# A feed-forward block in seven-product form: weight sums written as additions, part of them done by accumulating DMA

## The chip, the cores and the metric

One core of one Trainium2 chip runs the whole kernel. The metric is the device time in microseconds (us) of one execution; shorter is better. The engines are named as in the profile: PE (TensorE, matmuls), DVE (VectorE), ACT (ScalarE), POOL (GpSimd), SP (SyncE, which here only issues DMAs). A DMA that adds to what lies at its destination (accumulating DMA) is issued from POOL.

## The reference

A decoder layer over 1024 tokens of width 1024, in float32. What matters here is its last third:

```python
x = x + y @ w_out
h = rmsnorm(x, ffn_norm_g)
x = x + (silu(h @ w_gate) * (h @ w_up)) @ w_down     # 1024 -> 2816 -> 1024
return rmsnorm(x, final_norm_g)
```

Every operand of a matmul is split into a high part (rounded to the float32r format of PE) and a low part (the rest), and three matmuls high*high, high*low, low*high replace one in float32.

## The kernel before

**Seven products instead of eight.** The products `h @ w_gate` and `h @ w_up` are cut in blocks of two by two: rows in two halves of 512, the inner width in two halves, and two column blocks of 128 of the weight. The 2816 columns give 11 such pairs of blocks (`HF` = 11, index `j`), each once for gate and once for up (`m`). Each pair is done with seven block products instead of eight. That needs sums and differences of the weight blocks a11, a12, a21, a22 and of the row blocks. Class `Seven` (L694) does it: `load_part` loads the raw blocks (tile `wr`: half `kh` = 0 holds a11 and a21, half 1 holds a12 and a22), `mix` (L733) makes the weight sums on POOL, `prep` (L747) makes the high and low part of one operand (tile `wl`; high by ACT, low by DVE, in `split`, L160 and L161), and `run` (L772) issues the 12 matmuls of one product and combines its result on ACT or DVE. For a pair, `mix` computes

```python
add(s[:, 0, k], a21[:, k], a22[:, k], eng_)          # operand of product 5
sub(s[:, 1, k], s[:, 0, k], a11[:, k], eng_)         # operand of product 6
sub(a21[:, k], a11[:, k], a21[:, k], eng_)           # operand of product 7
```

(tile `sm` is `s`), and `prep` of product 7 takes `s[:, 1]` from a12 in place, which is product 3's operand. The products stand in the order 1, 6, 2, 7, 5, 4, 3; for the first two pairs it is 1, 2 of pair 0, 1, 2 of pair 1, then 6, 7, 5, 4, 3 of pair 0, then of pair 1 (`head`, L1489). In the trace product 6 is `fb<-t2h,wl`, 7 is `fb<-t3h,wl`, 5 `fa<-t1h,wl`, 4 `fb<-t4h,wl`, 3 `fa<-b22h,wl`, 1 `fa<-b11h,wl` and 2 `fa<-b21h,wl`. After product 7 the sum in `s[:, 1]` is no longer needed and its place takes an intermediate result (`sm<-fb,pu`).

**The rows.** The normalized rows come in eight blocks of 128; `to_h` (L1428) transposes a block and, for blocks 4 to 7, forms the differences with blocks 0 to 3: `r[:, 0]` (t1), `t23` (t2 and t3), and `r[:, 1]` (t4; tile `hraw`), the last by a POOL subtraction. `rest` inside it and `late_split` (L1556) make their high and low parts.

**What sets the order.** From L1606 to L1673 PE, DVE, ACT and POOL run in the order in which the code is written (`manual_schedule`); after that, and for SP throughout this stretch, a scheduler orders the instructions. The written order interleaves `prep_to(n)` (operands up to number n), `run()`, and the row work:

```python
    for i in range(1, 5):
        late_split(i - 1)
        if i == 2:
            ffn.prep_to(11)
        if i == 3:
            ffn.prep_to(12)
        ffn.run()
    ffn.prep_to(14)
    ffn.mix(1)
```

Tiles `wr`, `wl`, `sm`, `wd`, `act`, `hraw` and `t23` share 21 slots of 4 KB per partition (`U`); the raw weights of pairs 1 and up lie in slots of 8 KB (`V`). `wd_out` (L1508) loads blocks of `w_down`, forms differences on POOL and stores them; `act_out` (L1493) does the same with the activations.

Of the kernel before, what the change touches and what calls it, by code (L numbers as in the profile page):

```python
# [89 lines left out]
def hybrid_block_kernel(  # L90
# [603 lines left out]
    class Seven:  # L694


        def __init__(self, pairs, ms, load, done, ahead, load_at, mix_at, head=(), at=None, scale=None, scale_at=(), piece=4):
# [109 lines left out]
    def load_gate(j, kh):  # L807
        t = U("wr", F32, (P, 4, 2, P))
        nc.sync.dma_start(t, w_gt[j, kh])
        return {"g": t}  # L810

    def scale_gate(j, kh, k, raw):
        t = raw["g"]
        g = gT[:, 4 * kh + k:4 * kh + k + 1]
        if j == 0:
            nc.vector.tensor_scalar(t[:, k], t[:, k], g, None, op0=ALU.mult)  # L816
        else:
            nc.scalar.activation(t[:, k], t[:, k], AF.Copy, scale=g)
# [658 lines left out]
    def ffn_done(j, m, ps, f, sh, other):  # L1477
# [3 lines left out]
        if other is not None:  # L1481
            add(other, ps, other, nc.vector)
# [3 lines left out]
        else:  # L1486
# [383 lines left out]
```

## Time and profile before

| | |
|---|---|
| times of three runs | 1359.94, 1364.36, 1359.34 us, median 1359.94 |
| the profiled execution | 1360.19 us, its span 1358.4 us |
| PE | 1331.8 us busy, 98% of the span |
| DVE / ACT / POOL | 944.6 / 653.4 / 596.2 us, 70% / 48% / 44% |
| granted PE clock | 0.999 of full speed |

The span runs from the first to the last instruction; the execution's time has 1.8 us more around it. A matmul's end is modelled, so the pace of PE is read from the starts of matmuls. A row of a timeline gives start, duration, engine, line, operation, output and inputs, and in brackets the idle time of the engine just before it and what ended it.

### The profile page before, as it was taken

Reading aid. Unit: us, or ns where it says so; the run is one execution under the profiler, and the core shown is the slowest. Engines: PE = TensorE matmul, PEld = TensorE weight load, DVE = VectorE, ACT = ScalarE, POOL = GpSimd, SP = SyncE. Lnnn points to the kernel's source line nnn. Section 1 sums busy time; section 2 is a strip of 40 time slices with the busy share of each in tenths; the row PEclk is TensorE's granted clock in tenths of the full one; section 3 lists DMA queues with packets and bytes.
Section 4 is the critical chain, followed back from the end, with each engine's and each line's share of the span. In section 5 each row is a group of like instructions: output and inputs, shape, how many; then the busy total and the mean of one; then the engine's idle time right before and its main releaser. Section 6 shows DMA issues by size and latency. Waiting matters only on the chain.

```text
span 1358.4 us, 18967 instructions
## 1 busy us (share of the span) xinstructions
PE 1331.8 (98%) x6552; PEld 1112.0 (82%) x6552; DVE 944.6 (70%) x1527; ACT 653.4 (48%) x1317; POOL 596.2 (44%) x636
## 2 busy tenths in 40 slices
PE   9999999999999999999999999999999999999997
PEld 6899878878788888888887788888888888888886
DVE  6868767776777887489878866666656664664862
ACT  7433667665567777654357232322332332644452
POOL 1115545553066555131045875766665541022521
PEclk9999999999999999999999999999999999999999
DMA  9454332335100111598041353645444425996503
GB/s 360 161 182 154 115 106 82 98 121 174 71 2 13 43 32 32 219 307 264 31 171 62 112 188 140 227 178 178 147 153 165 163 85 184 379 385 237 171 16 140
DMA packets 78239, 205.39 MB, mean 151 GB/s; under 512 B 8768, under 2 KB 15424, under 8 KB 77504
## 3 DMA queue, kind: packets, MB, share of 16 engines
q1 hardware_dynamic: 76848, 199.99, 41.5%
q0 software_dynamic: 1152, 4.19, 1.6%
q8 instruction: 52, 0.85, 0.3%
q14 instruction: 43, 0.35, 0.1%
q10 hardware_dynamic: 144, 0.00, 0.0%
HBM read 141.24 MB, written 59.77 MB: 148 GB/s over the span
## 4 chain that ended last, share of the span: by engine, by line
PE 72%; DVE 7%; ACT 4%; issue 3%; POOL 3%; DMA 0%; POOLq 0%; ACTq 0%; DVEq 0%
PE fa L169 7%; PE fa L167 7%; PE fa L168 7%; PE fd L168 5%; PE fd L167 5%; PE fd L169 5%; PE fb L167 5%; PE fb L169 5%; PE fb L168 5%; DVE wl L161 2%; PE pTb L1161 2%; PE xo L167 1%; PE xo L168 1%; PE xo L169 1%; PE oA L167 1%
## 5 line engine op out<-in xcount | busy, mean ns | idle before, releaser
L161 DVE TENSOR_TENSOR wl<-wr,wl 128x512 fp32r<-128x512 f32 x150 | 154.6, 1052 | 75.4 <-ACT wl L160 75.1
L161 DVE TENSOR_TENSOR lrv<-lr,lrv 128x1024 fp32r<-128x1024 f32 x77 | 105.0, 1396 | 49.7 <-ACT lrv L160 47.1
L160 ACT CAST lrv<-lr 128x1024 fp32r<-128x1024 f32 x77 | 80.1, 1052 | 96.3 <-PE fd L169 56.0
L169 PE MATMUL fd<-lrv 128*128 128x512 f32 x308 | 119.9, 389 | 0.0
L168 PE MATMUL fd<-lrv 128*128 128x512 f32 x308 | 119.9, 389 | 0.0
L167 PE MATMUL fd<-lrv 128*128 128x512 f32 x308 | 119.9, 389 | 0.0
L172 POOL TENSOR_TENSOR wr<-wr,sm 128x512 f32<-128x512 f32 (+1 forms) x38 | 46.8, 1241 | 121.2 <-DVE wl L161 115.1
L160 ACT CAST wl<-wr 128x512 fp32r<-128x512 f32 x150 | 87.3, 623 | 3.1 <-DVE wr L816 2.6
L161 DVE TENSOR_TENSOR wl<-sm,wl 128x512 fp32r<-128x512 f32 x60 | 55.2, 946 | 45.4 <-ACT wl L160 45.4
L295 POOL TENSOR_SCALAR ms<-ss 128x1 f32<-128x1 f32 x32 | 9.8, 305 | 140.4 <-ACT xn L1582 62.5
L1146 POOL TENSOR_TENSOR denb<-denb,neg_one 128x1 f32<-128x1 f32 x64 | 36.4, 570 | 75.0 <-ACT p L1145 64.3
L167 PEld LDWEIGHTS fd<-lrv 128*128 128x128 f32 x308 | 57.8, 188 | 12.1
L169 PEld LDWEIGHTS fd<-lrv 128*128 128x128 f32 x308 | 57.8, 188 | 12.0
L168 PEld LDWEIGHTS fd<-lrv 128*128 128x128 f32 x308 | 57.8, 188 | 11.9
L1145 ACT ACTIVATE p<-scb,nmb 128x384 f32<-128x384 f32 (+3 forms) x64 | 47.5, 743 | 36.8 <-DVE nmb L1144 35.0
L161 DVE TENSOR_TENSOR ptl<-pTb,pth 128x512 fp32r<-128x512 f32 (+2 forms) x96 | 50.0, 549 | 13.6 <-ACT pth L160 12.8
L1144 DVE CUSTOM_DVE_ANT_0 scb<-scb,mask 128x384 f32<-128x384 f32 (+3 forms) x64 | 48.5, 758 | 14.1 <-PE scb L1136 13.7
L1485 ACT ACTIVATE act<-sm 128x512 f32<-128x512 f32 x11 | 7.0, 633 | 103.7 <-DVE sm L175 103.7
L1147 POOL TENSOR_SCALAR p<-p,denb 128x384 f32<-128x384 f32 (+3 forms) x64 | 49.1, 768 | 6.3
L1485 ACT ACTIVATE act<-pu 128x512 f32<-128x512 f32 x22 | 13.9, 632 | 74.8 <-DVE pu L175 74.8
L160 ACT CAST pth<-pTb 128x512 fp32r<-128x512 f32 (+2 forms) x96 | 42.9, 482 | 13.5 <-PE pTb L1161 12.9
L169 PE MATMUL fa<-t1h,wl 128*128 128x512 f32 x120 | 46.8, 391 | 2.6 <-DVE wl L161 2.6
(354 smaller groups left out, 4374.8 us busy)
## 6 DMA issues: line engine op xcount, KB each, us to landing
lr<-la_d SPq DMA_DIRECT2D x77, 256.0 KB, 5.4
wr<-in_w_gate_dram SPq DMA_DIRECT2D x22, 512.0 KB, 4.3
wr<-in_w_up_dram SPq DMA_DIRECT2D x22, 512.0 KB, 5.0
wd<-in_w_down_dram SPq DMA_DIRECT2D x22, 512.0 KB, 6.4
rb_d<-wd SPq DMA_DIRECT2D x22, 512.0 KB, 2.6
la_d<-sd SPq DMA_DIRECT2D x22, 512.0 KB, 4.8
lr<-rb_d SPq DMA_DIRECT2D x44, 256.0 KB, 5.4
lr<-in_w_down_dram SPq DMA_DIRECT2D x33, 256.0 KB, 5.6
```

Of the source, the lines that this page charges most:

```text
L160: nc.scalar.copy(hi, src)
L161: (eng or nc.vector).tensor_tensor(lo, src, hi.bitcast(F32), op=ALU.subtract)
L167: nc.tensor.matmul(ps, ah, bh, start=first and i == 0, stop=False, skip_group_check=go_on)
L168: nc.tensor.matmul(ps, ah, bl, start=False, stop=False, skip_group_check=go_on)
L169: nc.tensor.matmul(ps, al, bh, start=False, stop=last and i == n - 1, skip_group_check=go_on)
L172: eng.tensor_tensor(out, a, b, op=ALU.subtract)
L1144: nc.vector.tensor_tensor_reduce(s_, s_, m_, 1.0, -NEG, op0=ALU.add, op1=ALU.min, accum_out=nm)
L1145: nc.scalar.activation(p_, s_, AF.Exp, scale=-1.0, bias=nm, accum_out=den)
L1146: nc.gpsimd.tensor_tensor(den, den, neg_one[:, 0:1], op=ALU.pow)
L1147: nc.gpsimd.tensor_scalar(p[:, 0:w], p[:, 0:w], den, 0.0, op0=ALU.mult, op1=ALU.add)
L1161: nc.tensor.transpose(pp[:, i], p[:, blk(k0 + i)], ident)
L1485: nc.scalar.activation(dst, src, AF.Silu)
```

## The change

In the feed-forward block (`plus=True`) every weight sum is written as an addition: s1 = (a21 + a22) + a11, a21 + a11, a12 + s1. The signs move to the rows' operands and to the combinations of results. Accumulating DMAs then do a part of the work: (1) `r[:, 1]` of the row blocks 4 to 7; (2) for pair 0 (its mix stays on POOL) the sums a12 + s1; (3) for pair 1 all sums: SP loads a21 from DRAM into both halves of `sm`, then a22 and a11 are added from DRAM, and s1 to a12 from SBUF. Pairs 2 to 10 keep POOL. The weights' layout is changed so that a block is contiguous in a partition, for the feed-forward block and for the gates, which use the same class. The calls are put in another order.

```diff
     class Seven:
...
         def part(self, j, m, kh, f):
             self.load_part(j, kh)
             self.scale_part(j, kh)
-            return self.raws[(j, kh)][m][:, :, f]
+            return self.raws[(j, kh)][m][:, f]
...
                 for k in range(0, 4, n):
                     k = slice(k, k + n)
                     add(s[:, 0, k], a21[:, k], a22[:, k], eng_)
-                    sub(s[:, 1, k], s[:, 0, k], a11[:, k], eng_)
-                    sub(a21[:, k], a11[:, k], a21[:, k], eng_)
+                    op(s[:, 1, k], s[:, 0, k], a11[:, k], eng_)
+                    op(a21[:, k], a11[:, k], a21[:, k], eng_)
+
+        def mix_load(self, j):
+
+            for m in self.ms:
+                s = self.sums[(j, m)] = U("sm", F32, (P, 2, 4, P))
+                for i in range(2):
+                    nc.sync.dma_start(s[:, i], self.src[m][j, 0][:, 1])
+
+        def mix_sum(self, j, step):
+
+            def plus(dst, src):
+                nc.gpsimd.dma_start(dst, src, accum_op=ALU.add)
+
+            for m in self.ms:
+                a11, a22 = self.src[m][j, 0][:, 0], self.src[m][j, 1][:, 1]
+                s = self.sums[(j, m)]
+                if step == 0:
+                    for i in range(2):
+                        plus(s[:, i], a22)
+                elif step == 1:
+                    plus(s[:, 1], a11)
+                    plus(self.part(j, m, 0, 1), a11)
+                else:
+                    plus(self.part(j, m, 1, 0), s[:, 1])
...
-            if q == 7:
+            if q == 7 and j not in self.by_dma:
...
-                add(u2, ps, p1, nc.vector)
+                add(u2, ps, p1, nc.vector) if not self.plus else sub(u2, p1, ps, nc.vector)
...
     def to_h(pss, b):
...
-        sub(r[:, 0], pss[0], r[:, 0], nc.vector)
-        sub(t23[:, 0], pss[1], r[:, 0], nc.vector)
-        nc.scalar.copy(hq["t2"][0][:, :, blk(c)], t23[:, 0])
-        sub(r[:, 1], r[:, 1], t23[:, 0], nc.gpsimd)
+        sub(r[:, 0], r[:, 0], pss[0], nc.vector)
+        nc.vector.scalar_tensor_tensor(t23[:, 0], pss[1], -1.0, r[:, 0], op0=ALU.mult, op1=ALU.subtract)
+        nc.scalar.activation(hq["t2"][0][:, :, blk(c)], t23[:, 0], AF.Copy, scale=-1.0)
+        nc.gpsimd.dma_start(r[:, 1], t23[:, 0], accum_op=ALU.add)
...
+            nc.vector.scalar_tensor_tensor(t2l, t23[:, 0], -1.0, t2h.bitcast(F32), op0=ALU.mult, op1=ALU.subtract)
...
     for i in range(1, 5):
         late_split(i - 1)
-        if i == 2:
-            ffn.prep_to(11)
-        if i == 3:
-            ffn.prep_to(12)
+        if i == 1:
+            ffn.mix_sum(0, 2)
+        ffn.prep_to(9 + i + (i > 1))
+        if i == 4:
+            ffn.mix_load(1)
         ffn.run()
     ffn.prep_to(14)
-    ffn.mix(1)
+    ffn.mix_sum(1, 0)
+    ffn.run()
+    ffn.prep_to(15)
+    ffn.mix_sum(1, 1)
+    ffn.run()
+    ffn.prep_to(16)
+    ffn.mix_sum(1, 2)
     in_order.__exit__(None, None, None)
     ffn.n_ahead = 4
+    wd_out(0)
...
-        return m.reshape(2, 4, P, 2, n, P).transpose(4, 0, 2, 1, 3, 5)
+        return m.reshape(2, 4, P, 2, n, P).transpose(4, 0, 2, 3, 1, 5)
```

**How the order moves, on DVE** around products 6 to 5 of pair 0 (`t1l`: low parts of row blocks 0 to 3; `wl<-wr_7324` and `wr_7325`: product 7; `wl<-sm_7445` and `sm_7517`: product 5; `wl<-wr_7349` and `wr_7350`: product 4; gate first, then up). Before:

```order
L161 TENSOR_TENSOR t1l_7901<-hraw_7547,t1h_7900 128x4x128
L161 TENSOR_TENSOR wl_7927<-wr_7324,wl_7927 128x512
L175 TENSOR_TENSOR pu_7727<-fb_7930,pu_7727 128x512
L161 TENSOR_TENSOR t1l_7901<-hraw_7592,t1h_7900 128x4x128
L161 TENSOR_TENSOR wl_7949<-wr_7325,wl_7949 128x512
L175 TENSOR_TENSOR sm_7445<-fb_7908,pu_7707 128x512
L161 TENSOR_TENSOR t1l_7901<-hraw_7634,t1h_7900 128x4x128
L161 TENSOR_TENSOR wl_7997<-wr_7349,wl_7997 128x512
L161 TENSOR_TENSOR wl_8000<-wr_7350,wl_8000 128x512
L175 TENSOR_TENSOR sm_7517<-fb_7930,pu_7727 128x512
L161 TENSOR_TENSOR wl_7982<-sm_7445,wl_7982 128x512
L161 TENSOR_TENSOR wl_7985<-sm_7517,wl_7985 128x512
```

Now, with what each waits for (DMASW4 is the accumulating DMA that reads `sm_7445`, DMASW5 the one that reads `sm_7517`, DMASW3 that of the last `hraw`):

```order
L161 TENSOR_TENSOR t1l_7901<-hraw_7547,t1h_7900 128x4x128 [waits Activation_49]
L161 TENSOR_TENSOR wl_7928<-wr_7324,wl_7928 128x512 [waits Activation_49]
L161 TENSOR_TENSOR wl_7931<-wr_7325,wl_7931 128x512 [waits Activation_49]
L172 TENSOR_TENSOR pu_7727<-pu_7727,fb_7934 128x512 [waits PE_49]
L161 TENSOR_TENSOR t1l_7901<-hraw_7592,t1h_7900 128x4x128 [waits Activation_49]
L161 TENSOR_TENSOR wl_7952<-sm_7445,wl_7952 128x512 [waits DMASW3_49,Activation_49]
L172 TENSOR_TENSOR sm_7445<-fb_7910,pu_7707 128x512 [waits DMASW4_49,PE_49]
L161 TENSOR_TENSOR t1l_7901<-hraw_7634,t1h_7900 128x4x128 [waits Activation_49]
L161 TENSOR_TENSOR wl_7972<-sm_7517,wl_7972 128x512 [waits Activation_49]
L172 TENSOR_TENSOR sm_7517<-fb_7934,pu_7727 128x512 [waits DMASW5_49,DVE_49,PE_49]
L172 TENSOR_TENSOR sm_7445<-sm_7445,fa_7998 128x512 [waits DVE_49,PE_49]
L161 TENSOR_TENSOR wl_8014<-wr_7349,wl_8014 128x512 [waits Activation_49]
```

Product 5's two operands now come before those of product 4; the overwriting of `sm` now also waits for a DMA, and the last `t1l` stands behind it.

**On POOL**, from the low parts of t4 on, before (the mix of pair 1 is `sm_7988`, `sm_7992`):

```order
L161 TENSOR_TENSOR t4l_7905<-hraw_7547,t4h_7904 128x4x128
L172 TENSOR_TENSOR wr_7349<-wr_7349,sm_7445 128x4x128
L161 TENSOR_TENSOR t4l_7905<-hraw_7592,t4h_7904 128x4x128
L172 TENSOR_TENSOR wr_7350<-wr_7350,sm_7517 128x4x128
L161 TENSOR_TENSOR t4l_7905<-hraw_7634,t4h_7904 128x4x128
L175 TENSOR_TENSOR sm_7988<-wr_7521,wr_7566 128x512
L172 TENSOR_TENSOR sm_7988<-sm_7988,wr_7521 128x512
L172 TENSOR_TENSOR wr_7521<-wr_7521 128x4x128
L175 TENSOR_TENSOR sm_7992<-wr_7521,wr_7566 128x512
L172 TENSOR_TENSOR wr_7566<-wr_7566,sm_7988 128x4x128
L172 TENSOR_TENSOR sm_7992<-sm_7992,wr_7521 128x512
L172 TENSOR_TENSOR wr_7521<-wr_7521 128x4x128
```

Now (the sums of pair 1 are `sm_7975`, `sm_7978`):

```order
L761 DMA wr_7349<-sm_7445 128x512
L761 DMA wr_7350<-sm_7517 128x512
L161 TENSOR_TENSOR t4l_7905<-hraw_7547,t4h_7904 128x4x128
L161 TENSOR_TENSOR t4l_7905<-hraw_7592,t4h_7904 128x4x128
L161 TENSOR_TENSOR t4l_7905<-hraw_7634,t4h_7904 128x4x128
L761 DMA sm_7975<-in_w_gate_dram 128x512 x2
L761 DMA sm_7978<-in_w_up_dram 128x512 x2
L761 DMA sm_7975<-in_w_gate_dram 128x512
L761 DMA wr_7521<-in_w_gate_dram 128x512
L761 DMA sm_7978<-in_w_up_dram 128x512
L761 DMA wr_7521<-in_w_up_dram 128x512
L761 DMA wr_7566<-sm_7975 128x512
```

The arithmetic between the `t4l` and after them has become DMAs, the first two directly behind the first `t4l`; POOL goes through them in this order.

## Rows read from the trace of the kernel before

**Rows 1.** The page, busy time, share of the span and instructions of each engine.

```profile
PE 1331.8 (98%) x6552; PEld 1112.0 (82%) x6552; DVE 944.6 (70%) x1527; ACT 653.4 (48%) x1317; POOL 596.2 (44%) x636
```

**Rows 2.** What PE waited for, 690 to 830 us: total us, times, longest.

```profile
PE fa L169 <- DVE wl L161: 2.6, 1, 2.6
PE fb L169 <- DVE wl L161: 1.6, 2, 1.2
```

**Rows 3.** Timeline of PE: first matmuls of products and those after a wait.

```profile
737.25 0.49 PE L167 MATMUL fb<-t2h,wl 128*128 128x512 f32 x1
738.50 0.50 PE L168 MATMUL fb<-t2l,wl 128*128 128x512 f32 x1 [0.77 <-DVE t2l L172]
...
745.75 0.50 PE L169 MATMUL fb<-t3h,wl 128*128 128x512 f32 x1 [1.24 <-DVE wl L161]
...
755.90 0.50 PE L169 MATMUL fa<-t1h,wl 128*128 128x512 f32 x1 [2.61 <-DVE wl L161]
...
776.62 0.47 PE L167 MATMUL fb<-t3h,wl 128*128 128x512 f32 x1 [0.24 <-DVE pu L175]
...
798.50 0.39 PE L167 MATMUL fa<-b11h,wl 128*128 128x512 f32 x1
...
803.94 0.39 PE L167 MATMUL fb<-t2h,wl 128*128 128x512 f32 x1
```

**Rows 4.** Timeline of DVE in the same stretch.

```profile
725.45 0.67 DVE L172 TENSOR_TENSOR t2l<-t,t2h 128x512 fp32r<-128x512 f32 x1
...
737.23 1.22 DVE L172 TENSOR_TENSOR t2l<-t,t2h 128x512 fp32r<-128x512 f32 x1
...
742.83 1.18 DVE L161 TENSOR_TENSOR t1l<-hraw,t1h 128x512 fp32r<-128x512 f32 x1
743.93 1.76 DVE L161 TENSOR_TENSOR wl<-wr,wl 128x512 fp32r<-128x512 f32 x1
...
750.72 3.47 DVE L161 TENSOR_TENSOR wl<-wr,wl 128x512 fp32r<-128x512 f32 x2
...
754.71 2.84 DVE L161 TENSOR_TENSOR wl<-sm,wl 128x512 fp32r<-128x512 f32 x2
```

**Rows 5.** Timeline of POOL in the same stretch.

```profile
731.59 1.30 POOL L172 TENSOR_TENSOR hraw<-hraw,t 128x512 f32<-128x512 f32 x1 [3.22 <-DVE t L172]
...
740.32 3.15 POOL L161 TENSOR_TENSOR t4l<-hraw,t4h 128x512 fp32r<-128x512 f32 x2 [0.26 <-ACT t4h L160]
...
761.17 1.74 POOL L172 TENSOR_TENSOR wr<-wr,sm 128x512 f32<-128x512 f32 x1
...
775.35 1.66 POOL L175 TENSOR_TENSOR sd<-act,act 128x512 f32<-128x512 f32 x1 [5.63 <-DVE act L1487]
```

**Rows 6.** DVE by line and shape, 560 to 690 us: count, busy us, mean ns.

```profile
L161 DVE TENSOR_TENSOR wol<-wo,woh 128x1024 fp32r<-128x1024 f32 x10 | 12.1, 1218 | 0.2 <-ACT woh L160 0.2
...
L1364 DVE SCALAR_TENSOR_TENSOR wol<-wo,woh 128x1024 fp32r<-128x1024 f32 x4 | 4.9, 1219 | 0.0
```

**Rows 7.** The eight accumulating DMAs of 512 KB at L1352: issues, and landing.

```profile
593.55 0.86 POOL L1352 DMA_DIRECT2D wo<-in_w_out_dram  x1 [8.29 <-DMA wo<-wo]
597.44 0.89 POOL L1352 DMA_DIRECT2D wo<-in_w_out_dram  x1 [3.02 <-DMA wo<-wo]
...
DMA to landing us min/median/max: 7.9/9.8/13.0
```

**Rows 8.** Two stretches: busy of PE, PEld, DVE, ACT, POOL; clock, DMA share, GB/s.

```profile
590.00:595.00 5.00, 5.00 (x24) 4.14 (x23) 2.93 (x6) 4.02 (x5) 0.86 (x1) 1.00 1.08 261
...
740.00:750.00 10.00, 8.38 (x36) 6.28 (x35) 10.00 (x11) 6.59 (x13) 9.74 (x7) 1.00 0.43 142
```

**Rows 9.** The DMA issues: size of each and median us to landing.

```profile
la_d<-act SPq DMA_DIRECT2D x11, 256.0 KB, 3.2
```

**Rows 10.** Timeline of ACT: the high part for product 6 (up).

```profile
738.57 0.63 ACT L160 CAST wl<-sm 128x512 fp32r<-128x512 f32 x1
```

**Rows 11.** Timeline of SP: the load of pair 2's raw weights (up).

```profile
742.08 0.45 SPq L1474 DMA_DIRECT2D wr<-in_w_up_dram  x1
```

More of the change, by code (lines that the diff above doesn't have):

```diff
@@ L694, in hybrid_block_kernel, with __init__ @@
     class Seven:
-        def __init__(self, pairs, ms, load, done, ahead, load_at, mix_at, head=(), at=None, scale=None, scale_at=(), piece=4):
+        def __init__(self, pairs, ms, load, done, ahead, load_at, mix_at, head=(), at=None, scale=None, scale_at=(), piece=4, plus=False, src=None, by_dma=()):
             self.pairs, self.ms, self.load, self.done = pairs, ms, load, done
@@ L715, in __init__ @@
             self.piece = piece
+            self.plus = plus
+            self.src = src
             self.raws, self.sums, self.left, self.acc, self.tmp = {}, {}, {}, {}, {}
+            self.by_dma = set(by_dma)
         def load_part(self, j, kh):
@@ L740, in mix @@
                 eng_, n = (eng, 4) if eng is not None else (nc.gpsimd, self.piece)
+                op = add if self.plus else sub
                 for k in range(0, 4, n):
@@ L756, in prep @@
                     k = slice(k, k + self.piece)
-                    sub(a12[:, k], a12[:, k], s1[:, k], nc.gpsimd)
+                    (add if self.plus else sub)(a12[:, k], a12[:, k], s1[:, k], nc.gpsimd)
             t = U("wl", F32R, (P, 2, 4, P))
@@ L794, in run @@
             elif q == 6:
-                add(u2, ps, p1, nc.vector)
+                add(u2, ps, p1, nc.vector) if not self.plus else sub(u2, p1, ps, nc.vector)
             elif q == 7:
-                add(u3, ps, p1, nc.vector)
+                (sub if self.plus else add)(u3, ps, p1, nc.vector)
             else:
@@ L807, in load_gate @@
     def load_gate(j, kh):
-        t = U("wr", F32, (P, 4, 2, P))
+        t = U("wr", F32, (P, 2, 4, P))
         nc.sync.dma_start(t, w_gt[j, kh])
@@ L815, in scale_gate @@
         if j == 0:
[L816 removed]
+            nc.vector.tensor_scalar(t[:, :, k], t[:, :, k], g, None, op0=ALU.mult)
         else:
[L818 removed]
+            nc.scalar.activation(t[:, :, k], t[:, :, k], AF.Copy, scale=g)
     def gate_done(j, m, ps, f, sh, other):
@@ L1468, in load_w @@
         if j == 0:
-            t = [U("wr", F32, (P, 4, 2, P)) for _ in range(2)]
+            t = [U("wr", F32, (P, 2, 4, P)) for _ in range(2)]
         else:
-            v = V("wr", F32, (P, 2, 4, 2, P))
+            v = V("wr", F32, (P, 2, 2, 4, P))
             t = [v[:, 0], v[:, 1]]
@@ L1481, in ffn_done @@
         if other is not None:
-            add(other, ps, other, nc.vector)
+            if (f, sh) == (1, 1):
+                sub(other, other, ps, nc.vector)
+            else:
+                (add if sh else sub)(other, ps, other, nc.vector)
         src = ps if other is None else other
@@ L1490, in hybrid_block_kernel @@
     ffn = Seven(HF, "gu", load_w, ffn_done, 4, (2, 7), 5, head,
-                {(1, 6): [("load", 2, 0)], (1, 7): [("load", 2, 1)], (1, 5): [("mix", 2)]})
+                {(1, 6): [("load", 2, 0)], (1, 7): [("load", 2, 1)], (1, 5): [("mix", 2)]}, plus=True, src={"g": w_gate, "u": w_up},
+                by_dma=(0, 1))
     def act_out(j):
```

6 lines of the change are left out of this document (3 added, 3 removed).

## The prediction

> **What bounds the kernel now.** I read the page's busy table first: TensorE (PE) is busy 98% of the span, no other engine comes near [rows 1]. So only time in which PE stands still can be won. The summary of waits, cut to the stretch that the diff touches (690 to 830 us, the start of the feed-forward block), comes next: PE waits there mostly for VectorE (DVE), 2.6 us once and 1.6 us in two pieces, each time for `wl`, the low half of a weight tile [rows 2]. The timeline of PE then dates these waits and gives the loss without any model of a matmul's end [rows 3]. From 737.25 (product 6 of pair 0) to 776.62 (product 7 of pair 1) PE runs six groups of 24 matmuls (products 6, 7, 5, 4, 3 of pair 0 and 6 of pair 1, each for gate and up). The undisturbed pace stands in the same group: 803.94 - 798.50 = 5.44 us. Six groups need 32.64 us, took 39.37, so **6.73 us** are lost. That is the ceiling of the gain. The printed waits are 0.77, 1.6, 2.61 and 0.24, 5.2 in all; the other 1.5 us is the restart after each of the five, 0.3 apiece.
>
> Why is DVE late? Its timeline has two answers [rows 4]. A subtraction with both inputs in SBUF over 512 columns takes 0.67 us at one time and 1.18, 1.22 or 1.76 at others; the long ones lie beside POOL work [rows 5], for POOL computes nearly without a gap from 740.32 to 762.9. And the order is bad: two `wl` from `wr` (3.47 us, product 4) are done at 750.72, before the two from `sm` (product 5) at 754.71, though PE needs product 5 first and stands until 755.90.
>
> **What changes on the path, step by step.**
>
> Layout of the weights (`pairs`, tile shapes): the same bytes per load, the same element counts per instruction; nothing. The swapped operand signs: the same instruction on the same shapes; nothing. PE's own list changes by three matmuls of product 4 that no longer stand inside product 5; no matmul is added.
>
> The rows' part. Three TENSOR_TENSOR/CAST forms become scaled ones, four times each. Row against row, the scalar_tensor_tensor on 128x1024 takes 1219 ns where the plain subtraction on the same tile pair takes 1218 [rows 6]: nothing. [...]
>
> The four POOL subtractions on `hraw` (1.30 us each, [rows 5]) become accumulating DMAs; POOL pays 0.9 us to issue one [rows 7]. DVE's `t2l` of the last row block lies beside one of them: 1.22 us, against 0.67 for the same instruction at 725.45 alone [rows 4]. So it is done 0.54 us earlier, and the wait at 738.50 falls from 0.77 to 0.23.
>
> The mix of pair 1 (six POOL instructions), its two differences and the two differences of pair 0 leave POOL: ten instructions of 1.3 to 1.74 us, about 15 us up to 762.9 [rows 5]. In their place POOL issues 12 DMAs, and SP four plain loads. POOL keeps four `t4l`. What DVE gains: in `t1l` at 742.83 and `wl` at 743.93 the excess goes, since POOL then issues DMAs: 0.60 each between starts. That `wl` is done about 744.1 instead of 745.7. PE, 0.54 earlier itself, asks for it at 743.8: of the 1.24 us [rows 3] 0.2 remains, and the next `wl` follows at 744.7, long before it is due, so the second piece of the 1.6 goes.
>
> The order on DVE: the new order has `wl` of product 5 (gate) before `sm` and before any `wl` of product 4, so the 2.61 us wait loses its cause. **What is late next**: the last `t1l` (row block 3), which product 5 needs at its second matmul, now stands behind `sm<-fb,pu`, and that instruction overwrites the first sums of pair 0 and must await the accumulating DMA that reads them. Queued behind it are that `t1l` and `wl` of product 5 (up), and PE waits for both. The DMA is issued after the first `t4l`, near 742.0 [rows 5]; product 5's second matmul is due at 749.35 (743.8 + 0.2 wait, then the rest of products 7 at 0.227 us a matmul). With `sm` and `t1l` at 0.6 to 0.7 each, the DMA must land by 748.0.
>
> So all hangs on **L**, the time from issue to landing of an accumulating DMA of 256 KB. The trace has eight of 512 KB: 7.9 / 9.8 / 13.0 us [rows 7], while the 16 DMA engines were full (share 1.08, [rows 8]). The second of a pair frees its reader 3.9 us after the first (597.44 - 593.55, [rows 7]), so half the bytes take about 2 us less: 7.9 at the median. From below, a plain 256 KB store of this block lands in 3.2 us [rows 9]; and the engines are less than half full here (0.43 at 740 to 750, [rows 8]). Between 3.2 and 9.8 I take **L = 6**, nearer the accumulating rows. It then lands at 748.0, `t1l` at 749.3 to 749.8: a wait of up to 0.5, I count 0.4.
>
> [...]
>
> Three more places wait on L. The cast of product 6 (up) on ACT, at 738.57 [rows 10], now also waits for the third `hraw` DMA, issued where POOL did its subtraction, 731.6: slack 7.0, hidden at L = 6. The last `hraw` DMA is waited for about as long after its issue: hidden too. The sums of pair 1 form a chain: SP loads `sm` behind the loads of pair 2, the last issued at 742.08 [rows 11], POOL reaches the first accumulation after its last `t4l`, near 748.5, the gate's second one at 749.4, then `+= a11` when that has landed. Two L after 749.4, plus 0.7 for the cast, against product 6 of pair 1 due at 765.8 (749.5 plus three groups of 5.44): hidden up to L = 7.8. The differences on `wr` are read two to four groups later: hidden. POOL's `wd` work, which waits behind the last of these DMAs, ends some 5 us later than before; POOL then stood idle 5.63 us until its next job at 775.35 [rows 5], so this is covered.
>
> The sum: left over are 0.23 + 0.2 + 0.4 of waits and three restarts of 0.3, 1.7 us; 6.73 - 1.7 = **5.0 us** gained. After 776.62 nothing waits in this stretch, and the weights come ahead of need, so the gain lasts. The profiled execution took 1360.19 us (span 1358.4), so 1355.2; the median of the runs is 0.25 lower, 1354.9. I say **1355.0 us**.
>
> **Rivals.**
> 1. *Everything hides.* L near 3 to 4, and the remaining bits vanish: the whole 6.73 us, **1353.2**. For it: the DMA engines are lightly loaded. Against it: no accumulating row under 7.9.
> 2. *The DMA takes the place of POOL.* L between 8 and 11.6. At 9.8 the ACT cast slips by 2.8, with it the first `t4l` and the issue of the differences (744.8), these land at 754.6, `t1l` at 756.0; product 5 starts near 755.8, product 6 of pair 1 at 772.1 to 772.5 (the chain of sums ends there too), product 7 at 777.9 against 776.62: **1.3 us slower, 1361**. For it: the median of the rows; against: those engines were full.
> 3. *Slower for certain.* The same mechanism at the row's maximum, L = 13: `t1l` at 762.4, sums of pair 1 at 782, product 7 at 787.5, **10.9 us slower, 1371**. Between the two points it costs 3 us for each us of L, so it crosses +0.5% at L = 11.6.
> 4. *DVE does not get faster.* The change doesn't do what it says, because issuing DMAs on POOL slows DVE as its arithmetic did (or the new forms are slow after all). Then only the order helps, the 2.61 us wait: **1357.3**. Against it: DVE's `wol` kept 1218 ns in a stage in which POOL issued DMAs, though not at the same moment that I can show.
>
> **How the numbers follow.** A measurement of this kernel can tell about 0.5% (6.8 us) from no change: below 1353.1 faster, above 1366.7 slower. Forecast (gain 3.4 to 6.1, L from 4 to 8) 0.55, its own range 1353.8 to 1356.6; rival 1 0.12, half of it past the bound; rival 2 0.17; rival 3 0.04; rival 4 0.12. So faster 0.06, within 0.5% 0.90, slower 0.04. The range leaves out about a tenth at either end: 1352.9 (the ceiling and 0.3 for the runs) to 1361.3 (rival 2 at its median).
>
> **What would show it.** In PE's waits from 690 to 830 us: the 2.6 for `wl` gone, the 1.6 down to about 0.2, a new one of some 0.4 at product 5. `t2l` at 0.68 us, `wl` between 743 and 748 mostly 0.7, not 1.76. The accumulating DMAs landing in 5 to 7 us. Product 7 of pair 1 at 771 to 772 instead of 776.62. The prediction is wrong if PE waits several us at product 5 or at product 6 of pair 1 for a landing, or if DVE's times stay long.

## The result and the profile after

The changed kernel takes **1365.27 us** (median of 16 runs, 1363.24 to 1370.06); the kernel before took 1361.28 us beside it (16 runs). Ratio 1.0032, 95% interval [1.0022, 1.0043]: about 4 us slower. That is within the 0.5% which the prediction called no change, but a gain of 5.0 us had been forecast, and the time lies outside the range of 1352.9 to 1361.3.

The two profiled executions start product 6 of pair 0 at nearly the same moment, 737.25 before [rows 3] and 737.13 after. Product 7 of pair 1, where the forecast stretch ends, starts at 781.66 instead of 776.62 [rows 3], 5.0 us late, where 771 to 772 had been forecast. Product 5 of pair 1, one group later, is 7.1 us late, and the distance stays: product 6 of pair 2 starts at 803.94 before [rows 3] and 811.06 after. So all of the loss of these two executions lies between; it is 7.2 us, while the medians over 16 runs differ by 4.0. PE's waits from 690 to 830 us, after (total us, times, longest):

```profile
PE fb L167 <- DVE pu L172: 4.7, 1, 4.7
PE fb L169 <- DVE wl L161: 4.5, 1, 4.5
PE fa L167 <- ACT pu L821: 0.4, 1, 0.4
PE fb L168 <- DVE t2l L1486: 0.2, 1, 0.2
```

Against [rows 2] and [rows 3]: the 2.6 is gone and the 0.77 is down to 0.2, as forecast, and two new waits of 4.5 and 4.7 us are there. PE's timeline, after (start, duration, engine, line, operation; in brackets the idle time before and what ended it), dates them:

```profile
743.22 0.39 PE L167 MATMUL fb<-t3h,wl 128*128 128x512 f32 x1
743.45 0.39 PE L168 MATMUL fb<-t3l,wl 128*128 128x512 f32 x1
748.30 0.55 PE L169 MATMUL fb<-t3h,wl 128*128 128x512 f32 x1 [4.47 <-DVE wl L161]
748.65 0.63 PE L167 MATMUL fb<-t3h,wl 128*128 128x512 f32 x1
749.08 0.63 PE L168 MATMUL fb<-t3l,wl 128*128 128x512 f32 x1
...
755.02 0.39 PE L167 MATMUL fa<-t1h,wl 128*128 128x512 f32 x1
...
771.34 0.39 PE L167 MATMUL fb<-t2h,wl 128*128 128x512 f32 x1
...
781.66 0.76 PE L167 MATMUL fb<-t3h,wl 128*128 128x512 f32 x1 [4.72 <-DVE pu L172]
782.22 0.63 PE L168 MATMUL fb<-t3l,wl 128*128 128x512 f32 x1
...
789.30 0.39 PE L167 MATMUL fa<-t1h,wl 128*128 128x512 f32 x1
```

From product 6 of pair 0 to product 5 of pair 1 stand seven groups of 24 matmuls, 38.08 us at the undisturbed pace of 5.44. Before they took 44.93 (737.25 to 782.18), after 52.17 (737.13 to 789.30), so 14.1 us are lost instead of 6.85. They split by the starts: 0.65 in product 6 of pair 0, 6.36 in its product 7 (11.80 instead of 5.44), nothing in products 5, 4 and 3, 4.88 in product 6 of pair 1 with the wait behind it, 2.20 in its product 7. A wait here costs more than itself. Behind both, the spacing of matmuls is 0.43 us (748.65 to 749.08) instead of 0.23, and the view of stretches shows why (busy us of PE, PEld, DVE, ACT, POOL; granted PE clock; DMA share; GB/s):

```profile
745.00:750.00 5.00, 1.70 (x5) 1.35 (x6) 5.00 (x6) 0.32 (x1) 2.09 (x2) 0.86 1.07 268
750.00:755.00 5.00, 5.00 (x19) 4.02 (x18) 2.55 (x5) 0.00 (x0) 2.64 (x3) 0.80 1.09 333
780.00:785.00 5.00, 3.34 (x8) 2.69 (x9) 3.19 (x5) 0.61 (x2) 4.61 (x4) 0.50 0.77 274
```

After each stand of over 4 us (4.47 and 4.72) the granted clock was at half (0.50 from 780 to 785 us) for some microseconds, with matmuls 0.43 us apart until 751.64 and until 786.06: 1.9 us on top of the first wait (6.36 - 4.47) and 2.4 on top of the second (4.88 + 2.20 - 4.72). Before, the clock was 1.00 throughout this stretch, the 2.61 us wait included. The last column but one says something else that is new: the DMA engines are full (1.07 and 1.09). In the same two windows before they stood at 0.27 and 0.56:

```profile
745.00:750.00 5.00, 3.87 (x16) 2.90 (x17) 5.00 (x6) 1.59 (x3) 5.00 (x4) 1.00 0.27 92
750.00:755.00 5.00, 3.29 (x15) 2.39 (x13) 5.00 (x5) 0.00 (x0) 4.92 (x4) 1.00 0.56 188
```

**The first wait.** DVE and POOL, after, two timelines:

```profile
737.12 0.69 DVE L1486 SCALAR_TENSOR_TENSOR t2l<-t,t2h 128x512 fp32r<-128x512 f32 x1
...
742.72 4.93 DVE L161 TENSOR_TENSOR t1l<-hraw,t1h 128x512 fp32r<-128x512 f32 x1
747.57 1.28 DVE L161 TENSOR_TENSOR wl<-wr,wl 128x512 fp32r<-128x512 f32 x2
...
769.60 2.42 DVE L161 TENSOR_TENSOR wl<-sm,wl 128x512 fp32r<-128x512 f32 x1 [3.51 <-ACT wl L160]
771.94 1.78 DVE L161 TENSOR_TENSOR wl<-wr,wl 128x512 fp32r<-128x512 f32 x1
...
775.34 1.77 DVE L1519 TENSOR_TENSOR act<-pu,act 128x512 f32<-128x512 f32 x1
...
780.83 0.68 DVE L172 TENSOR_TENSOR pu<-pu,fb 128x512 f32<-128x512 f32 x1
```

```profile
741.59 1.77 POOL L761 DMA_DIRECT2D wr<-sm  x2
742.73 4.36 POOL L161 TENSOR_TENSOR t4l<-hraw,t4h 128x512 fp32r<-128x512 f32 x3
750.77 0.88 POOL L761 DMA_DIRECT2D sm<-in_w_gate_dram  x1 [3.68 <-DVE wl L161]
...
756.13 0.86 POOL L761 DMA_DIRECT2D sm<-in_w_up_dram  x1 [2.08 <-issue]
...
769.26 0.88 POOL L761 DMA_DIRECT2D wr<-sm  x1 [1.27 <-DMA sm<-in_w_up_dram]
769.83 1.64 POOL L172 TENSOR_TENSOR wd<-wd 128x512 f32<-128x512 f32 x1
771.54 3.32 POOL L172 TENSOR_TENSOR wd<-wd,wd 128x512 f32<-128x512 f32 x2
```

`t2l` is at 0.69, as forecast. But the second `t1l`, 1.18 in [rows 4], takes 4.93. It starts 0.01 us before POOL's second `t4l` and ends 0.56 after the end of the fourth (742.73 + 4.36 = 747.09): it ran behind the whole row. The `wl` for which PE stood came after it.

**The second wait.** Product 7 of pair 1 writes the tile `fb` that held product 6, and PE began it at 781.66, behind 4.72 us of waiting for DVE's reading of that tile (`pu<-pu,fb`, at 780.83). On DVE ten instructions stand in the order between `wl<-sm` (up) and that one, and they begin when the last sum of pair 1 has landed, 769. At the same moment POOL turns to `wd`, and several of them take 1.2 to 2.4 us instead of 0.68.

### The profile page after: what moved, and what is told of

Same layout as the page of the kernel before. It is cut to its first block, busy times and chain, and to the rows that moved or that the text cites. A ratio compares the mean times of both kernels' runs of the same rounds, so it can differ in the third digit from the quotient of the medians.

```text
span 1364.8 us, 19004 instructions
## 1 busy us (share of the span) xinstructions
PE 1333.3 (98%) x6552; PEld 1113.6 (82%) x6552; DVE 939.7 (69%) x1527; ACT 653.8 (48%) x1317; POOL 585.6 (43%) x638
## 5 line engine op out<-in xcount | busy, mean ns | idle before, releaser
L161 DVE TENSOR_TENSOR wl<-wr,wl 128x512 fp32r<-128x512 f32 x150 | 148.5, 1012 | 75.8 <-ACT wl L160 75.4
L161 DVE TENSOR_TENSOR wl<-sm,wl 128x512 fp32r<-128x512 f32 x60 | 51.6, 885 | 50.5 <-ACT wl L160 50.4
L175 POOL TENSOR_TENSOR wr<-wr,sm 128x512 f32<-128x512 f32 x18 | 26.7, 1482 | 110.0 <-DVE wl L161 110.0
L167 PE MATMUL fb<-t3h,wl 128*128 128x512 f32 x120 | 49.1, 409 | 4.7 <-DVE pu L172 4.7
L169 PE MATMUL fb<-t3h,wl 128*128 128x512 f32 x120 | 48.3, 403 | 4.5 <-DVE wl L161 4.5
```

The lines of the kernel that those rows point to most:

```text
L161: (eng or nc.vector).tensor_tensor(lo, src, hi.bitcast(F32), op=ALU.subtract)
L167: nc.tensor.matmul(ps, ah, bh, start=first and i == 0, stop=False, skip_group_check=go_on)
L169: nc.tensor.matmul(ps, al, bh, start=False, stop=last and i == n - 1, skip_group_check=go_on)
L175: eng.tensor_tensor(out, a, b, op=ALU.add)
```

## The experiments

T7 in what follows is the time from product 6 of pair 0 to product 5 of pair 1 in the profiled execution, read from PE's timeline as above (undisturbed 38.08). One execution of a kernel differs from the next by some us elsewhere, so T7 shows the mechanism and the ratio, over several runs, the size. T7 also begins behind the rows' part: PE's wait for `pu` just ahead of product 6 of pair 0 is 1.1 us before, in order_alone and in candidate_no_dma, and 0.4 to 0.5 in the kernels whose rows are summed by DMA.

| kernel | T7 | ratio to before, 95% interval |
|---|---|---|
| before | 44.93 | 1 |
| changed | 52.17 | 1.0032 [1.0022, 1.0043] |
| order_alone | 46.54 | 1.001 [0.9999, 1.0021] |
| t4l_on_dve | 49.23 | 1.0033 [1.0019, 1.0046] |
| pair1_on_pool | 48.41 | 1.0017 [1.0006, 1.0028] |
| pair0_on_pool | 49.83 | 1.0021 [1.0011, 1.0032] |
| dma_before_t4l | 52.53 | 1.005 [1.0029, 1.007] |
| dma_after_t4l | 52.06 | 1.0044 [1.0027, 1.006] |
| wd_later | 42.57 | 0.9988 [0.9977, 0.9999] |
| wd_later_only | 45.68 | 0.999 [0.9979, 1.0001] |
| pair1_on_dve | 42.23 | 0.9975 [0.9962, 0.9989] |
| both_on_dve_wd_later | 39.95 | 0.996 [0.9946, 0.9974] |
| candidate_no_dma | 41.56 | 0.9972 [0.9961, 0.9984] |
| dma_earlier_wd_later | 42.42 | 0.995 [0.9934, 0.9965] |

The first four asked whether the second wait is a consequence of the first (theory A) or has a cause of its own (B: the chain of sums by DMA is too long).

**t4l_on_dve.**

```diff
-            split_h(name, c, r[:, i], (nc.vector, nc.gpsimd)[i])
+            split_h(name, c, r[:, i], nc.vector)
```

> The changed kernel with the four t4l subtractions on DVE instead of POOL; nothing else moves. Theory A (the loss starts where POOL runs three t4l without a pause and DVE's t1l stands 4.93 us beside them; everything later, the late slot for the sums of pair 1 and the second wait of 4.7 us, follows from that): DVE gets 4 x 0.6 us more work and never stands; its t1l and t4l take 0.7 each, SP's load of the second sums goes out about 744 instead of 748.3, the chain of accumulating DMAs ends about 4 us earlier, the wait before product 7 of pair 0 falls from 4.5 to at most 1.5 and the wait of 4.7 before product 7 of pair 1 to under 1.5: 5 to 9 us faster than the changed kernel, ratio to the kernel before 0.996 to 0.999. Theory B (the chain of the sums of pair 1, load, += a22, += a11, is too long by itself): the first wait falls as in A, but product 7 of pair 1 still waits 4 us or more: ratio 0.9995 to 1.002.

PE's waits in it, 690 to 830 us:

```profile
PE fb L167 <- DVE pu L172: 6.9, 1, 6.9
PE fb L169 <- DVE wl L161: 0.9, 1, 0.9
```

The first wait fell to 0.9: POOL's `t4l` were its cause. Product 6 of pair 1 started 29.05 us after product 6 of pair 0 (33.53 before), a gain of 4.5 us, almost what had been forecast. Then the second wait took it all back, 6.9 us instead of 4.7, though SP issued the loads of the second sums at 743.54 instead of 748.28. A fell for the second wait. The ratio, 1.0033, is that of the changed kernel and lies outside what either theory gave; T7 is 2.9 us shorter than in the changed kernel, which the ratio doesn't show: this execution, 1362.66 us, is the fastest of its ten (median 1365.22).

**pair1_on_pool** (`by_dma=(0,)`; the mix of pair 1 and the end of the written order as before):

```diff
-        if i == 4:
-            ffn.mix_load(1)
...
-    ffn.mix_sum(1, 0)
-    ffn.run()
-    ffn.prep_to(15)
-    ffn.mix_sum(1, 1)
-    ffn.run()
-    ffn.prep_to(16)
-    ffn.mix_sum(1, 2)
+    ffn.mix(1)
...
-    wd_out(0)
```

> The changed kernel with the sums of pair 1 and its a12 differences computed on POOL again, as in the kernel before; pair 0's differences and the rows' hraw stay accumulating DMAs. Both theories: the wait of 4.5 us before product 7 of pair 0 stays, since the three t4l still stand in a row. A: the second wait goes because POOL needs no slot from DVE's late work and no landing: ratio about 1.000 (0.999 to 1.001). B: the same second wait goes, 4.7 to 7 us, since the chain is gone: ratio 0.998 to 1.000. What it tells is the price of the pair 1 chain as such: under A no more than what t4l_on_dve wins at that place, under B all of it here and none there.

The second wait is gone (product 7 of pair 1 exactly 5.44 us behind product 6), but the first grew from 4.5 to 6.8, and T7 has 3.3 us beyond the undisturbed pace and the waits (48.41 - 38.08 - 7.0): the mix now stood directly behind the `t4l`, and the `t1l` took 6.13 us. So the ratio is worse than B and A wanted. It also put `wd` back to where it ran before, so it cannot tell the chain from `wd`.

**pair0_on_pool** (`by_dma=(1,)`):

```diff
-        if i == 1:
-            ffn.mix_sum(0, 2)
```

> The changed kernel with the two a12 differences of pair 0 as POOL subtractions again (they stand between the second and the third t4l, so that POOL runs t4l, t4l, wr, wr, t4l, t4l); pair 1's sums stay accumulating DMAs. A1 (what stops DVE is any gap-free run of POOL arithmetic): DVE's t1l stands 5 us or more and the time is as that of the changed kernel or slower, ratio 1.002 to 1.006. A2 (it was the particular place: t4l and t1l started within 0.01 us of each other behind two DMA issues on POOL; in the kernel before, DVE got in between POOL's instructions, 1.2 to 1.8 us each): t1l takes 1.2 to 1.8, the wait before product 7 of pair 0 is 1 to 2 us, but POOL reaches the accumulating DMAs of pair 1 near 750 as now, so the second wait stays near 4: ratio 1.000 to 1.002.

A2 held in its first part: POOL ran t4l, t4l, wr, wr, t4l, t4l without a gap, and DVE got in between (`t1l` 1.18, two `wl` 3.44); first wait 1.8. So this gap-free row on POOL did not lock DVE out. The second wait stayed, 5.3.

**order_alone** (an edit of the kernel before):

```diff
-        if i == 2:
-            ffn.prep_to(11)
-        if i == 3:
-            ffn.prep_to(12)
+        ffn.prep_to(9 + i + (i > 1))
```

> The kernel before with nothing changed but the order in which weight tiles are prepared among the last four row blocks (product 5 of pair 0 ahead of product 4, as in the changed kernel). The prediction's step on the order (the 2.61 us wait of product 5 goes, about 2.9 us with its restart): ratio 0.998. If the order gains nothing, because the next tile is late instead: ratio 1.000.

The 2.6 for product 5 is gone, but a wait of 1.2 for `t1l` at the same product and one of 2.3 for `pu` before product 7 of pair 1 (0.24 before) stand in its place; the 1.3 for `wl` at product 7 of pair 0 is there as before. The order alone wins nothing that can be measured: it hands the lateness on, since DVE has as much to do as before and beside the same POOL work.

**What the lockout needs.** Two kernels move pair 0's two DMAs.

```diff
     for i in range(1, 5):
+        if i == 1:
+            ffn.mix_sum(0, 2)
         late_split(i - 1)
-        if i == 1:
-            ffn.mix_sum(0, 2)
```

> The changed kernel with the two accumulating DMAs of pair 0 issued ahead of the first t4l instead of between the first and the second; POOL then runs four t4l in a row. A2 (DVE stands because the DMA issues are directly ahead of a t4l, at which DVE's t1l is let go in the same moment): the t1l beside the second and third t4l take 1.2 us and the first wait is 1.5 us or less; the second stays at 4 to 7; ratio 1.000 to 1.002. A1 (three or more t4l in a row stop DVE whatever stands ahead): a t1l of 4 us or more, first wait 4 us or more; ratio 1.003 as the changed kernel.

dma_after_t4l has `if i == 4` in the place of `if i == 1`. There the DMAs read `sm[:, 1]` after product 7's result has overwritten it, so the operand of product 3 of pair 0 has other contents.

> The changed kernel with pair 0's two accumulating DMAs issued behind the fourth t4l: POOL runs four t4l in a row with no DMA issue ahead of them. If the DMA issues are what lets DVE be locked out, every t1l takes 0.7 to 1.2 us and the first wait is under 1.5 us, but the last t1l and product 5 wait 2 to 4 us for the later landing: ratio 1.002 to 1.005. If a row of t4l by itself does it: a t1l of 4 us or more again, ratio 1.004 to 1.008.

DVE and POOL in dma_before_t4l:

```profile
740.38 6.19 DVE L161 TENSOR_TENSOR t1l<-hraw,t1h 128x512 fp32r<-128x512 f32 x1
...
739.26 1.75 POOL L761 DMA_DIRECT2D wr<-sm  x2
740.42 5.60 POOL L161 TENSOR_TENSOR t4l<-hraw,t4h 128x512 fp32r<-128x512 f32 x4
```

and in dma_after_t4l:

```profile
742.88 1.19 DVE L161 TENSOR_TENSOR t1l<-hraw,t1h 128x512 fp32r<-128x512 f32 x1
...
744.59 1.18 DVE L161 TENSOR_TENSOR t1l<-hraw,t1h 128x512 fp32r<-128x512 f32 x1
745.70 3.44 DVE L161 TENSOR_TENSOR wl<-wr,wl 128x512 fp32r<-128x512 f32 x2
...
742.06 6.53 POOL L161 TENSOR_TENSOR t4l<-hraw,t4h 128x512 fp32r<-128x512 f32 x4 [0.25 <-ACT t4h L160]
```

The same four `t4l` in a row: behind DMA issues they shut DVE out for their whole length (a `t1l` of 6.19 us beside 5.60 of `t4l`), without them DVE got in between (1.19 and 1.18 beside 6.53). So dma_before_t4l came out as A1 had it, and dma_after_t4l took away A1's "whatever stands ahead". A row of POOL subtractions directly behind a DMA issue locked DVE out in all four kernels that had it with t1l in place (changed, pair1_on_pool, wd_later_only, dma_before_t4l: 4.93, 6.13, 4.94, 6.19 us) and in none of four without it (before, pair0_on_pool, dma_after_t4l, dma_earlier_wd_later: 1.19 at most for a `t1l`). Two things stay open. In the four locked cases `t1l` and the first `t4l` of the row also start within 0.04 us of each other, while in the four others each `t1l` beside the row starts 0.8 to 1.1 us after a POOL instruction began; no run separates the DMA issue from this coincidence. And a DMA issue directly ahead is not enough: in the changed kernel the four `wd` subtractions stand behind one too (769.26), and the two `wl` beside them took 2.42 and 1.78 us, not the 6.7 us of that row (one issue stands ahead there, two in the locked cases). The trace has 0.08 us of idle time between those subtractions and none between the `t4l`; in pair1_on_pool the lockout ended at the first such gap, ahead of the second instruction of the mix (746.65). Why POOL keeps its turn, the runs don't show. In dma_after_t4l DVE then waited 6.3 us for the landing of the late DMAs, and the loss expected from them came (1.0044).

**What the second wait needs.** Three kernels start from t4l_on_dve or the changed kernel. wd_later is t4l_on_dve with

```diff
     ffn.n_ahead = 4
-    wd_out(0)
...
+        if (j, q, m) == (1, 7, "u"):
+            wd_out(0)
```

> The kernel t4l_on_dve with the loads and the four POOL subtractions of wd for pair 0 put behind product 7 of pair 1. In t4l_on_dve the six DVE instructions from 765.23 on take 2.42, 1.78, 1.17, 1.75 us beside these subtractions, 0.68 each without: an excess of 4.4 us. If it is this that holds product 7 of pair 1, its wait falls from 6.9 to about 2.5 us and, with less time at the lower clock, the ratio to the kernel before is 0.998 to 1.000. If the landing of the last sums holds it, DVE's ends hardly move: wait 5 us or more, ratio 1.002 to 1.003.

DVE in t4l_on_dve, from the last sum on, and then in wd_later:

```profile
765.23 2.42 DVE L161 TENSOR_TENSOR wl<-sm,wl 128x512 fp32r<-128x512 f32 x1 [2.86 <-ACT wl L160]
767.58 1.78 DVE L161 TENSOR_TENSOR wl<-wr,wl 128x512 fp32r<-128x512 f32 x1
...
776.43 0.68 DVE L172 TENSOR_TENSOR pu<-pu,fb 128x512 f32<-128x512 f32 x1
```

```profile
765.17 0.69 DVE L161 TENSOR_TENSOR wl<-sm,wl 128x512 fp32r<-128x512 f32 x1 [3.73 <-ACT wl L160]
765.78 0.68 DVE L161 TENSOR_TENSOR wl<-wr,wl 128x512 fp32r<-128x512 f32 x1
...
772.42 1.28 DVE L172 TENSOR_TENSOR pu<-pu,fb 128x512 f32<-128x512 f32 x2
```

The same sum at the same time, and the instruction that PE waits for comes 4.0 us earlier; the wait falls from 6.9 to 2.4, as expected, and the ratio from 1.0033 to 0.9988. POOL's four `wd` subtractions beside DVE's catching up were most of the second wait; the remaining 2.4 is the late sum.

The same edit on the changed kernel itself:

> The changed kernel with t4l left on POOL and only wd's loads and subtractions of pair 0 put behind product 7 of pair 1. If the two waits are separate, the first stays (about 4.5 us and 1.9 of half clock, product 5 of pair 0 near 18 us after product 6) and the second falls below 1.5 us, since DVE's queue behind the last sums then runs at 0.6 us an instruction: ratio to the kernel before 1.000 to 1.001. If the second wait is a consequence of the first (the late slot for the sums), it stays at 4 us or more: ratio 1.002 to 1.003.

The second wait is gone altogether, the first is as it was (4.5, with the clock at 0.71 and 0.60 in the two windows from 745 to 755 us): the two are separate. The ratio came out a little better than either line, 0.999, with an interval that just reaches 1.

pair1_on_dve is t4l_on_dve with pair 1's chain taken away instead, and leaves `wd`:

```diff
-        if i == 4:
-            ffn.mix_load(1)
...
     ffn.prep_to(14)
-    ffn.mix_sum(1, 0)
+    ffn.mix(1, nc.vector, "g")
     ffn.run()
     ffn.prep_to(15)
-    ffn.mix_sum(1, 1)
     ffn.run()
     ffn.prep_to(16)
+    ffn.mix(1, nc.vector, "u")
     ffn.mix_sum(1, 2)
```

> The kernel t4l_on_dve with pair 1's two sums and first difference (six instructions) on DVE instead of ten accumulating DMAs and four loads; the a12 differences of both pairs and the rows' hraw stay accumulating DMAs. In t4l_on_dve DVE idled 2.0, 1.3, 3.8 and 2.9 us between 749 and 765, and six sums need 4 us. If the second wait comes from the chain of accumulating DMAs (12 of 256 KB at about 160 GB/s, which keep the 16 DMA engines full from 741 to 765), it goes with them: product 6 of pair 1 starts about 29 us after product 6 of pair 0, product 7 of pair 1 about 5.5 us later, no granted clock under 1.0 in this stretch; gain against the kernel before 4 to 5.5 us, ratio 0.996 to 0.997. Rival: the second wait comes from POOL's wd subtractions beside DVE, now two groups earlier than in the kernel before; then a wait of 2 to 4 us stays, ratio 0.999 to 1.000.

The wait falls to 0.7, since DVE has the sums early and `wd` meets it with time to spare (two `wl` of 3.74 there, waits of 0.7 and 0.7); 0.9975 [0.9962, 0.9989], a little short of the 0.997 expected. So either half of the cause is enough to take away: the late chain or `wd` beside it.

**Versions that beat both kernels.** both_on_dve_wd_later joins the last two edits; candidate_no_dma makes its remaining eight accumulating DMAs POOL additions.

> The candidate: t4l and pair 1's sums on DVE, wd for pair 0 behind product 7 of pair 1; pair 0's and pair 1's a12 differences and the rows' hraw by accumulating DMA. In pair1_on_dve wd's subtractions still cost DVE 3.74 instead of 1.3 us for two wl and left waits of 0.7 and 0.7. Without them: product 7 of pair 1 about 34.0 us after product 6 of pair 0 (35.7 in pair1_on_dve, 39.4 in the kernel before): ratio 0.996 to 0.997. If wd's subtractions come into the way two groups later instead, no better than pair1_on_dve: 0.9975.

> The same as both_on_dve_wd_later, with the last eight accumulating DMAs (rows' hraw, a12 of both pairs) as POOL additions, so that no sum is made by a DMA. If what the DMAs win on DVE is real (t2l 0.69 instead of 1.22, no POOL arithmetic beside DVE's busiest ten microseconds), this is 1 to 3 us slower than the candidate: ratio 0.998 to 0.9985, with a wait before product 7 of pair 0 of 1 us or more and one of 0.8 for t2l. If the gain comes from the order and from DVE's own sums alone, it equals the candidate within 0.5 us.

The first has no wait above 0.9 and T7 = 39.95, 1.9 over the undisturbed pace. Without DMAs the waits of 1.0 and 0.7 (`t2l` at 1.22 again) return, and T7 is 1.6 longer. The ratios, 0.996 and 0.9972, lie the same way, but their intervals overlap. So what these eight DMAs are worth is not clear of the noise; T7 and the medians (1355.44 and 1357.46) put it near 2 us. A kernel without any sum by DMA is at 0.9972, better than the 0.998 expected: most of the gain of these two versions does not need the DMAs.

dma_earlier_wd_later keeps the change whole, all its sums by DMA and `t4l` on POOL, and moves two things:

```diff
     ffn.run()
+    ffn.mix_sum(0, 2)
     next_h()
...
-        if i == 1:
-            ffn.mix_sum(0, 2)
...
-    wd_out(0)
...
+        if (j, q, m) == (1, 7, "u"):
+            wd_out(0)
```

> The changed kernel, all of its sums by DMA and t4l on POOL, with two things moved: pair 0's two accumulating DMAs are issued one row block earlier, so that on POOL a subtraction that waits for ACT stands between them and the row of four t4l, and wd for pair 0 stands behind product 7 of pair 1. If DVE is locked out only where a row of POOL subtractions follows a DMA issue directly, no DVE instruction of the stretch takes over 2 us, the first wait is 1.0 to 1.9 us as in dma_after_t4l, the second under 2.5, the granted clock stays 1.0: product 5 of pair 1 about 42 to 43.5 us after product 6 of pair 0, ratio 0.997 to 0.999. If the row of t4l alone does it (dma_after_t4l was an accident of timing), a t1l of 4 us or more and a first wait of 4 us: ratio 0.999 to 1.000, as wd_later_only.

DVE and POOL in it:

```profile
739.44 1.19 DVE L161 TENSOR_TENSOR t1l<-hraw,t1h 128x512 fp32r<-128x512 f32 x1
...
741.15 1.19 DVE L161 TENSOR_TENSOR t1l<-hraw,t1h 128x512 fp32r<-128x512 f32 x1
742.26 3.44 DVE L161 TENSOR_TENSOR wl<-wr,wl 128x512 fp32r<-128x512 f32 x2
...
732.86 1.78 POOL L761 DMA_DIRECT2D wr<-sm  x2
...
738.62 6.52 POOL L161 TENSOR_TENSOR t4l<-hraw,t4h 128x512 fp32r<-128x512 f32 x4 [0.26 <-ACT t4h L160]
```

No lockout, a first wait of 1.8 as in dma_after_t4l, no second wait. One expectation failed: behind the 1.8 the clock did drop (0.72 from 745 to 750 us), and still the kernel is the fastest of all, 1354.41 us, 0.995 [0.9934, 0.9965], some 6.5 us better than before and 11 better than the change as it was, and better than the 0.997 to 0.999 expected. Its interval overlaps that of both_on_dve_wd_later. T7 shows 2.5 us of that gain. The profiled execution is 4.9 us shorter than the one before; 1.7 of that lie ahead of product 6 of pair 0 (735.57 instead of 737.25), a start that ranges from 735.4 to 740.9 over all the executions here. So most of the gain beyond T7 is not explained.

## Why the prediction was wrong

**Right.** The ceiling and its place; that the 2.61 us wait of product 5 would go (product 5 starts at 755.02 without a wait); `t2l` at 0.69 and its wait at 0.2; that the scaled form costs nothing (0.69 for scalar_tensor_tensor beside 0.68 for the plain form). The layout and the signs, which no run takes by themselves, show no cost: from product 5 of pair 1 to the end of the span it takes 575.5 us after and 576.2 before. A gain of the forecast size came only with further edits: both_on_dve_wd_later, where pair 1's sums are on DVE too, is 5.4 us better by its ratio (0.996) and 5.0 by T7, and dma_earlier_wd_later is at 0.995. That the size agrees does not confirm the sum, since the terms are others.

**Wrong, first step: "in `t1l` at 742.83 and `wl` at 743.93 the excess goes, since POOL then issues DMAs: 0.60 each".** POOL's two issues last 1.77 us, and behind them three `t4l` now stand in a row that had been spread between other instructions. The order showed it, and the text says that "POOL keeps four `t4l`", but it priced them at nothing. The excess did not go, it grew from 0.5 to 4.25 us. In the kernel before, the 1.18 us of the `t1l` at 742.83 end 0.54 after POOL's second `t4l` [rows 4, rows 5]: by these times it waited for the rest of one POOL instruction. The 4.93 goes beyond it: by the profile the DVE instruction started first, by 0.01 us, and it waited for three.

**Wrong, second step: POOL's `wd` work "ends some 5 us later than before", and since POOL then stood idle 5.63 us, "this is covered".** It was covered for POOL. What runs beside it on DVE was not asked. `wd` moved from 762.9 to 769.8, onto the ten DVE instructions between the last sum and the reading of product 6, and wd_later_only shows that this was the second wait.

**Wrong, third step: the sums of pair 1 are "hidden up to L = 7.8", against product 6 due at 765.8.** L = 6 was right as a middle (the medians of the groups from issue to landing are 3.3 to 6.6 us), but single DMAs took 3.3 to 9.2, and the two on which product 5 hung, pair 0's `wr<-sm`, were the slow ones:

```profile
DMA to landing us min/median/max: 7.8/8.5/9.2
```

They landed at 749.38 and 751.37, where the text wanted the first by 748.0. That nobody waited for them is luck: the first wait had delayed product 7, and DVE came to the overwriting of `sm` at 752.49 and waited there for PE. The reason given for a small L was wrong as well. The engines were "less than half full" before the change; the change fills them (1.07 and 1.09 above). The profile of the changed kernel, 736 to 775 us:

```profile
q0 software_dynamic: 1872, 3.41, 51.3%
q1 hardware_dynamic: 1397, 3.82, 30.1%
...
sm<-in_w_up_dram POOLq DMA_DIRECT2D x3, 256.0 KB, 6.6
...
sm<-in_w_gate_dram SPq DMA_DIRECT2D x2, 256.0 KB, 8.1
...
hraw<-t POOLq DMA_DIRECT2D x1, 256.0 KB, 3.3
```

The accumulating DMA that POOL issued at 736.83, with the engines at 0.30 from 735 to 740 us, landed in 3.3 us. Beside the others even SP's plain load took 8.1, and the chain began behind it: the gate's first accumulation was issued at 750.77 instead of 748.5, its second at 752.29 instead of 749.4. The gate's chain still ended in time, its sum landed at 764.66 and its cast began at 764.74, against 765.8. What the text did not price is the chain for up, which POOL issues in turn with the gate's: its last sum landed at 768.87, 4.2 us later, and the last cast on ACT came at 768.95. PE did not wait for it, because the first wait had delayed product 6 to 771.34; the DVE queue behind it did. The text asked when product 6 needs its operand, and not what is queued on DVE behind the low part of that operand.

**Not in the sum at all:** the clock. A restart of 0.3 us per wait was taken from waits up to 2.6 us; the waits of 4.5 and 4.7 cost 1.9 and 2.4 us beyond themselves.

**The rivals.** None had the mechanism. "DVE does not get faster" came nearest, but put it on the issuing of DMAs and priced it at a smaller gain; what holds DVE up is the arithmetic behind the issue (in wd_later, with no `t4l` behind the same two issues, the `t1l` beside them took 0.67), and the order by itself, to which it gave 2.6 us, gains nothing (order_alone, 1.001). Rivals 2 and 3 needed L of 8 or more. Pair 0's two DMAs came near that, and product 5 started at 755.02, near the 755.8 of rival 2, but behind the first wait and not behind a landing. Of the signs that the prediction gives for being wrong, the last one came: a time of DVE stayed long, 4.93 us for the `t1l`.

## What to carry to other kernels

When work leaves an engine, look at what then stands back to back on it, and at who runs beside each of its jobs at their new time; idle time of an engine covers its own delay and nobody else's (the first `wl` beside `wd` took 2.42 us). Where an engine keeps a written order, ask what stands behind the late instruction, up to the one that another engine waits for. The DMAs that took over arithmetic were not free where many did so at once (7.8 and 9.2 us to landing for pair 0's two, 3.3 for the one at a share of 0.30): size such a DMA with the engines as full as the change makes them.

## What the runs showed of the hardware

- In four kernels of four (changed, pair1_on_pool, wd_later_only, dma_before_t4l) a row of three or four `t4l` subtractions on POOL (in pair1_on_pool with an addition behind them), without a gap, directly behind DMA issues on POOL and begun within 0.04 us of a `t1l` on DVE, kept that `t1l` waiting for its whole length, 4.93 to 6.19 us. A row of the same `t4l` behind a wait for ACT, in which DVE came 0.8 us later (dma_after_t4l, dma_earlier_wd_later), left a `t1l` at 1.19 at most; and the `wd` row of the changed kernel, with 0.08 us between its subtractions, behind a DMA issue too, left a `wl` at 2.42.
- From 736 to 775 us of the changed kernel the accumulating DMAs kept the engines busy about twice as long for their bytes as the plain ones: 3.41 MB in 51.3% of 39 us (20.0 us, 170 GB/s) against 3.82 MB in 30.1% (11.7 us, 325 GB/s). POOL also stood up to 4.9 us between two issues where the trace shows nothing that it waited for (dma_before_t4l, ahead of the issue at 757.97; 2.1 in the changed kernel, at 756.13).
- In the windows during or just behind PE's stands of 4.2 us and more the granted clock fell to 0.86, 0.80 and 0.50 (changed, 4.47 and 4.72), to 0.71 and 0.60 (wd_later_only, 4.5) and to 0.50 twice (dma_before_t4l, 4.6 and 4.2). It also fell at stands of 3.3 and 2.9 (dma_after_t4l, 0.58 and 0.69), and in two profiled executions behind one of 1.8 (pair0_on_pool, 0.57; dma_earlier_wd_later, 0.72). It stayed at 1.00 behind a 1.8 in dma_after_t4l, the 2.4 in wd_later and the 2.61 of the kernel before: in these runs the length of a single stand does not decide it.
